# A two-layer diffusion block: modulation vectors of one stream, moved into the weights' load stream

## The chip, the cores and the metric

One core of a Trainium2 chip runs the whole program. The metric is device time in microseconds of that core, lower is better. The engines are named as in the profile: PE is TensorE (matmuls), PEld its weight loads, DVE is VectorE, ACT is ScalarE, POOL is GpSimd and SP is SyncE, which here only starts DMAs.

## The reference

Two layers over two streams of 256 tokens each, a latent stream x and a context stream, width 1024, all in float32. Each layer is FFN, mixer, FFN, and each of these three has a shift, a scale and a gate, nine modulation vectors of 1024 that are a matrix product of the conditioning vector with a large weight (ada_w):

```python
mod_x = (jax.nn.silu(c) @ ada_w[layer] + ada_b[layer]).reshape(b, N_MOD, 1, d)
mod_c = (jax.nn.silu(c_ctx) @ ada_w[layer] + ada_b[layer]).reshape(1, N_MOD, 1, d)
x = ffn_branch(x, mod_x, 0, norm_w[layer, 0], ffn_w1[layer, 0], ffn_w2[layer, 0])
ctx = ffn_branch(ctx, mod_c, 0, ...)
hx = ada_rms(x, norm_w[layer, 1], mod_x[:, 3], mod_x[:, 4])
hc = ada_rms(ctx, norm_w[layer, 1], mod_c[:, 3], mod_c[:, 4])
yx, yc = hybrid_mixer(hx, hc, ..., not last)
x = x + mod_x[:, 5] * yx
x = ffn_branch(x, mod_x, 6, norm_w[layer, 2], ffn_w1[layer, 1], ffn_w2[layer, 1])
if not last:
    ctx = ctx + mod_c[:, 5] * yc
    ctx = ffn_branch(ctx, mod_c, 6, ...)
```

The mixer is one input projection, three groups of heads (neighbourhood attention, a spatial gate, retention) and one output projection. Only x is returned. So in the last layer the vectors 5 to 8 (the mixer's gate, and shift, scale and gate of the last FFN) are needed for x alone.

## The kernel before

Activations lie transposed, feature on partitions, the two streams side by side in 512 columns. Every product is made of three matmuls of a high and a low part (wh, wl of the weights; hTh, hTl, aTh, aTl of the activations).

The weights come through one `Stream` (line 48): a list of chunks of up to 128x1024, in the order of their use. Three steps work along the list: `_load` starts a DMA on SP into one of three buffers `wr` (line 82), `_high` makes `wh` on ACT (line 92), and `_split` makes `wl` on DVE (line 103), whereupon the `wr` buffer is free. `take` hands a chunk to PE and then splits ahead until three chunks past it are split (`AHEAD`), and starts loads for three more. Instructions stand on each engine in the order in which the program is written (a manual schedule), so a step that waits holds what is written behind it on the same engine.

The first FFN of the first layer is called (0, 0) here, then come mixer 0, FFN (0, 1), FFN (1, 0), mixer 1 and FFN (1, 1). In an FFN each half has an up part (products `g`, `u`, some of them made by a faster scheme as `p`) and a down part (`d`). In a mixer the input projection has 28 chunks: three groups of four (`nat`, query, key and value), six `rqk`, then gates and spatial gate, and two `su` (in mixer 1 two chunks are swapped in order); 8 chunks of the output projection (`op`) follow.

The modulation vectors are 72 tiles of 128x1024 per layer (nine vectors by eight blocks). A tile is loaded by DMA and reduced on DVE against the conditioning vector `cb`, one multiply-and-sum per stream (line 293: a custom instruction and the reading of its sum); after eight blocks line 298 adds the bias, and where the vector is a scale or a half gate, one more small step follows. `ada_steps(l, count)` makes a list of such steps for as many reductions as `count` asks, and `pump`, called after each product, draws from that background list `bg` at a set pace. The table `ADA1` says how many reductions of the second layer stand in which FFN and half. For vectors 5 to 8 of the second layer a tile has one reduction, not two. There, in FFN (1, 0) and (1, 1), POOL starts the tiles' loads, into buffers of their own.

The mixers have background lists too: `qk_ticks` scales query and key (`qkn`, line 990) for PE's transposes (`qkt`, line 1003), attention follows (`sc`, `pt`, `o`), then retention, whose norm ends in POOL and DVE steps, and the spatial gate (`sg`). `windows` copies parts of the values on SP (`vW`, line 910), and mixer tables and biases are loaded on SP as well.

Of the kernel before, what the change touches and what calls it, by code (L numbers as in the profile page):

```python
# [43 lines left out]
ADA1 = {(0, 0): (40, 0), (0, 1): (16, 16), (1, 0): (16, 16), (1, 1): (8, 0)}  # L44
# [22 lines left out]
class Stream:  # L67
# [10 lines left out]
    def _load(self):  # L78
        i = self.n_load
        ap = self.chunks[i]  # L80
        t = self.pool.tile([128, CHUNK], F32, tag="wr", name="wr", bufs=RAW_BUFS)
        self.nc.sync.dma_start(out=t[:, : ap.shape[1]], in_=ap)
        self.raw[i] = t
        self.n_load += 1

    def _high(self):
        i = self.n_high
        if self.n_load <= i:
            self._load()
        h = self.pool.tile([128, CHUNK], F32R, tag="wh", name="wh", bufs=HL_BUFS)  # L90
# [5 lines left out]
    def _split(self):  # L96
        i = self.n_split
        n = self.chunks[i].shape[1]
        if self.n_high <= i:
            self._high()  # L100
        t, h = self.raw.pop(i), self.high.pop(i)
# [25 lines left out]
    def take(self, ahead=AHEAD):  # L127
        while self.n_split <= self.n_take:
            self._split()
# [8 lines left out]
def tile_hybrid_dit(ctx: ExitStack, tc: tile.TileContext, t_x, t_c, t_cb, t_ada0, t_ada, t_adab, t_nw, t_w1, t_w2,  # L138
# [83 lines left out]
    with tc.manual_schedule():  # L222
# [42 lines left out]
        ada_todo = [[(r, b) for r in range(2 if l == 0 else 0, 9) for b in range(KT)] for l in range(L)]  # L265

        def ada_steps(l, count):
# [3 lines left out]
            def streams(r):  # L271

                return 1 if l == L - 1 and r > 4 else 2

            todo = []
            while ada_todo[l] and sum(streams(r) for r, b in todo) < count:
# [11 lines left out]
            def step(i, s, n):  # L288
# [3 lines left out]
                junk = adap[3].tile([128, CHUNK], F32, tag="cu", name="junk", bufs=1) if s < n - 1 else t  # L292
                V.tensor_tensor_reduce(out=junk, in0=t, in1=cb[:, s], scale=1.0, scalar=0.0, op0=ALU.mult, op1=ALU.add,  # L293
                                       accum_out=mod[l][:, 8 * r + b, s:s + 1])

            def fin(r, n):
                mo = mod[l][:, 8 * r:8 * r + 8, 0:n]
                V.tensor_tensor(out=mo, in0=mo, in1=adab[:, l, 8 * r:8 * r + 8].unsqueeze(2).to_broadcast([128, KT, n]),
                                op=ALU.add)
                i, k = divmod(r, 3)  # L300
                if k == 1:
                    V.scalar_tensor_tensor(out=amul[l][:, i, :, 0:n], in0=mo, scalar=1.0,
                                           in1=nw[:, l, i, :].unsqueeze(2).to_broadcast([128, KT, n]),
                                           op0=ALU.add, op1=ALU.mult)
                elif k == 2 and i != 1:
                    V.tensor_scalar(out=mo, in0=mo, scalar1=0.5, scalar2=None, op0=ALU.mult)

            out = [lambda: loads(adap[1])]
            for i, (r, b) in enumerate(todo):
                n = streams(r)  # L310
                out += [lambda i=i, s=s, n=n: step(i, s, n) for s in range(n)]
                if b == KT - 1:
                    out.append(lambda r=r, n=n: fin(r, n))
# [324 lines left out]
        def ffn(l, f, lead, norms, steps=None, tail=None):  # L638
# [7 lines left out]
            with ExitStack() as es:  # L646
# [15 lines left out]
                else:  # L662
                    nb = ADA_BUFS - one
                    adap[:] = lambda i: fp.tile([128, CHUNK], F32, tag="aw", name="aw", bufs=nb), nb, G if one else SP, fp
                if one:
                    bg.extend([lambda: None] * 8 + ada_steps(1, ADA1[l, f][0]))
                    pace[0], pace[1] = len(bg) / (KT * (JH - 1)), 0.0
                for half in range(2):
# [121 lines left out]
                    if one and half == 0:  # L790
                        drain_bg()
# [1110 lines left out]
```

## Time and profile before

| | us |
|---|---|
| three timed runs | 1790.5, 1792.3, 1798.3 (median 1792.3) |
| the profiled execution | 1793.3 |
| its span in the trace | 1791.6 |
| PE busy | 1755.4 |
| DVE busy | 1294.0 |
| ACT busy | 719.1 |
| POOL busy | 257.1 |

The 1.7 us between the profiled execution and its span lie around the traced instructions. The granted TensorE clock was 0.998 of full speed over the span. PE's busy time counts a matmul from its start to its modelled end, so a PE that is always busy can still be fed slowly; waits are told apart in the rows further down, where a bracket at the end of a line holds the idle time before it and what ended it.

The stages by the trace: mixer 0 from 409 to 686 us, FFN (0, 1) to 1040, FFN (1, 0) to 1397, mixer 1 to 1590, FFN (1, 1) to the end.

### The profile page before, as it was taken

The page shows a single profiled execution, that of the slowest core. Times are in us where ns is not written, and L with a number is a line of the kernel's source. Part 1 is how long each engine was busy: PE and PEld are TensorE (multiplying, and loading weights), DVE is VectorE, ACT ScalarE, POOL GpSimd, SP SyncE. Part 2 cuts the span into 40 slices and gives each one's busy share as a digit, 9 for nine tenths or more (in the row PEclk, how much of TensorE's full clock was granted, in tenths as well). Part 3 has the DMA queues.
Part 4 walks back from the last instruction along what each step waited for, and adds up shares of the span by engine and source line. Part 5 has one row for each costly group of instructions (what it writes and reads, how often), then busy time and mean ns, then how long its engine had stood idle before and what let it go on. Part 6 is the DMA issues. An engine that isn't in the chain of part 4 may idle for free. (4 is left out here: it accounts for less than half of the span.)

```text
span 1791.6 us, 29394 instructions
## 1 busy us (share of the span) xinstructions
PE 1755.4 (98%) x11496; PEld 1544.3 (86%) x11496; DVE 1294.0 (72%) x2208; ACT 719.1 (40%) x1203; POOL 257.1 (14%) x307
## 2 busy tenths in 40 slices
PE   7999999999999999999999999999999999999999
PEld 5788888888678989898999899979998878899999
DVE  5789988986455567787688877776888745568665
ACT  3332222225544234442344244413542554454443
POOL 0000000002114400220322002113221105310000
PEclk9999999999999999999999999999999999999999
DMA  8756766644221122655775427567757432366655
GB/s 306 238 193 215 252 214 200 213 139 152 84 65 55 53 76 77 161 170 182 173 187 166 157 83 176 151 205 188 188 172 246 141 96 77 109 198 203 197 180 151
DMA packets 106811, 290.61 MB, mean 162 GB/s; under 512 B 12720, under 2 KB 22064, under 8 KB 106544
## 3 DMA queue, kind: packets, MB, share of 16 engines
q1 hardware_dynamic: 89392, 243.64, 41.9%
q0 software_dynamic: 17280, 45.10, 11.1%
q8 instruction: 90, 1.47, 0.3%
q14 instruction: 49, 0.40, 0.1%
HBM read 286.07 MB, written 1.05 MB: 160 GB/s over the span
## 5 line engine op out<-in xcount | busy, mean ns | idle before, releaser
L103 DVE TENSOR_TENSOR wl<-wr,wh 128x1024 fp32r<-128x1024 f32 (+2 forms) x308 | 325.7, 1083 | 108.3 <-ACT wh L92 107.2
L92 ACT CAST wh<-wr 128x1024 fp32r<-128x1024 f32 (+2 forms) x308 | 279.9, 934 | 185.1 <-PE d L210 88.9
L211 PE MATMUL d<-aTh,wl 128*128 128x512 f32 (+1 forms) x770 | 268.9, 349 | 2.5 <-DVE wl L103 2.5
L209 PE MATMUL d<-aTh,wh 128*128 128x512 f32 (+1 forms) x770 | 269.0, 349 | 0.7 <-ACT wh L92 0.7
L210 PE MATMUL d<-aTl,wh 128*128 128x512 f32 (+1 forms) x770 | 268.6, 349 | 0.0
L211 PEld LDWEIGHTS d<-aTh,wl 128*128 128x128 f32 x770 | 144.5, 188 | 24.6 <-DVE wl L103 3.5
L293 DVE CUSTOM_DVE_ANT_0 aw<-aw,cb 128x1024 f32<-128x1024 f32 x128 | 155.6, 1223 | 12.6 <-DMA aw<-in_ada_dram 9.9
L209 PEld LDWEIGHTS d<-aTh,wh 128*128 128x128 f32 x770 | 144.5, 188 | 22.1 <-ACT wh L92 0.9
L210 PEld LDWEIGHTS d<-aTl,wh 128*128 128x128 f32 x770 | 144.5, 188 | 21.2
L209 PE MATMUL g<-hTh,wh 128*128 128x512 f32 (+2 forms) x464 | 158.4, 341 | 2.1 <-ACT wh L92 1.1
L211 PE MATMUL g<-hTh,wl 128*128 128x512 f32 (+2 forms) x464 | 157.3, 339 | 2.0 <-DVE wl L103 2.0
L210 PE MATMUL g<-hTl,wh 128*128 128x512 f32 (+2 forms) x464 | 157.3, 339 | 1.3 <-DVE hTl L369 1.1
L211 PE MATMUL u<-hTh,wl 128*128 128x512 f32 (+2 forms) x464 | 156.4, 337 | 0.4 <-DVE wl L103 0.4
L209 PE MATMUL u<-hTh,wh 128*128 128x512 f32 (+2 forms) x464 | 156.1, 336 | 0.0
L210 PE MATMUL u<-hTl,wh 128*128 128x512 f32 (+2 forms) x464 | 156.1, 336 | 0.0
L217 PE MATMUL nat<-wh,hTh 128*128 128x512 f32 (+2 forms) x384 | 136.4, 355 | 0.0
L219 PE MATMUL nat<-wh,hTl 128*128 128x512 f32 (+2 forms) x384 | 128.4, 334 | 0.4 <-DVE hTl L369 0.4
L218 PE MATMUL nat<-wl,hTh 128*128 128x512 f32 (+2 forms) x384 | 128.3, 334 | 0.0
L293 DVE CUSTOM_DVE_ANT_0 junk<-aw,cb 128x1024 f32<-128x1024 f32 x96 | 117.0, 1219 | 4.0 <-DMA aw<-in_ada_dram 3.6
L595 PE MATMUL p<-hTh,wl 128*128 128x256 f32 x408 | 116.1, 285 | 0.7
L595 PE MATMUL p<-th,wl 128*128 128x256 f32 x408 | 114.7, 281 | 0.8 <-DVE wl L564 0.8
L594 PE MATMUL p<-hTl,wh 128*128 128x256 f32 x408 | 114.6, 281 | 0.0
(266 smaller groups left out, 4010.3 us busy)
## 6 DMA issues: line engine op xcount, KB each, us to landing
wr<-in_w_dram SPq DMA_DIRECT2D x142, 512.0 KB, 4.4
aw<-in_ada_dram SPq DMA_DIRECT2D x92, 512.0 KB, 4.9
wr<-in_wi_dram SPq DMA_DIRECT2D x56, 512.0 KB, 3.6
aw<-in_ada_dram POOLq DMA_DIRECT2D x52, 512.0 KB, 4.8
wr<-in_w_dram SPq DMA_DIRECT2D x64, 384.0 KB, 3.7
wr<-in_w_dram SPq DMA_DIRECT2D x64, 320.0 KB, 3.0
q<-in_w_dram SPq DMA_DIRECT2D x68, 256.0 KB, 3.7
q<-in_w_dram POOLq DMA_DIRECT2D x68, 256.0 KB, 5.3
```

Of the source, the lines that this page charges most:

```text
L92: self.nc.scalar.copy(out=h[:, :n], in_=self.raw[i][:, :n])
L103: self.nc.vector.tensor_tensor(out=lo[:, :n], in0=t[:, :n], in1=h[:, :n].bitcast(F32), op=ALU.subtract)
L209: PE.matmul(out=ps, lhsT=wh[:, col:col + 128], rhs=hh[rhs_sl], start=start, stop=False)
L210: PE.matmul(out=ps, lhsT=wh[:, col:col + 128], rhs=hl[rhs_sl], start=False, stop=False)
L211: PE.matmul(out=ps, lhsT=wl[:, col:col + 128], rhs=hh[rhs_sl], start=False, stop=stop)
L217: PE.matmul(out=ps, lhsT=hh[lhs_sl], rhs=wh[:, wc], start=start, stop=False)
L218: PE.matmul(out=ps, lhsT=hh[lhs_sl], rhs=wl[:, wc], start=False, stop=False)
L219: PE.matmul(out=ps, lhsT=hl[lhs_sl], rhs=wh[:, wc], start=False, stop=stop)
L293: V.tensor_tensor_reduce(out=junk, in0=t, in1=cb[:, s], scale=1.0, scalar=0.0, op0=ALU.mult, op1=ALU.add, accum_out=mod[l][:, 8 * r + b, s ...
L594: PE.matmul(out=ps, lhsT=wh[:, cw], rhs=tl, start=False, stop=False)
L595: PE.matmul(out=ps, lhsT=wl[:, cw], rhs=th, start=False, stop=n == 3)
```

## The change

The tiles of vectors 5 to 8 of the second layer become entries of the weights' stream. Behind each input projection chunk from the fourth on stands one such tile: 24 (vectors 5, 6, 7) in mixer 0, behind chunks 4 to 27, and 8 (vector 8) in mixer 1, behind chunks 4 to 11. An entry of this kind is loaded into a `wr` buffer by SP, has no ACT step, and in the place of the split it is reduced on DVE; `take` steps over it. They count in `AHEAD` and in the three buffers like any chunk. `ada_steps` now covers vectors 0 to 4 of the second layer alone; in `ADA1` FFN (1, 0) keeps 8 reductions (four tiles, both streams) in its first half and none in its second, and FFN (1, 1) has none. The work is the same in sum: 32 loads and 32 reductions have moved.

```diff
-ADA1 = {(0, 0): (40, 0), (0, 1): (16, 16), (1, 0): (16, 16), (1, 1): (8, 0)}
+ADA1 = {(0, 0): (40, 0), (0, 1): (16, 16), (1, 0): (8, 0)}
...
     def _load(self):
         i = self.n_load
         ap = self.chunks[i]
+        if isinstance(ap, tuple):
+            ap = ap[0]
...
     def _high(self):
...
+        if isinstance(self.chunks[i], tuple):
+            self.n_high += 1
+            return
...
     def _split(self):
         i = self.n_split
-        n = self.chunks[i].shape[1]
         if self.n_high <= i:
             self._high()
+        if isinstance(self.chunks[i], tuple):
+
+            self.chunks[i][1](self.raw.pop(i))
+            self.n_split += 1
+            return
...
     def take(self, ahead=AHEAD):
+        while isinstance(self.chunks[self.n_take], tuple):
+            self.split_to(1)
+            self.n_take += 1
...
+    between = [[(r, b) for r in v for b in range(KT)] for v in ((5, 6, 7), (8,))]
...
-                chunks += [t_wi[l, i] for i in WI[l]] + [t_wo[l, m] for m in range(KT)]
+                for n, i in enumerate(WI[l]):
+                    chunks.append(t_wi[l, i])
+                    if n >= 3 and between[l]:
+                        r, b = between[l].pop(0)
+                        chunks.append((t_ada[L - 1, r, b], lambda t, r=r, b=b: one_stream(r, b, t)))
...
+        def one_stream(r, b, t):
+            ada_step(L - 1, r, b, 0, t, t)
+            if b == KT - 1:
+                ada_fin(L - 1, r, 1)
...
-                if one:
-                    bg.extend([lambda: None] * 8 + ada_steps(1, ADA1[l, f][0]))
-                    pace[0], pace[1] = len(bg) / (KT * (JH - 1)), 0.0
```

PE's instructions and their order are the same in both. On SP, in mixer 1, around its first copies of values: `wr` buffers fed from `in_wi_dram` are weights, those from `in_ada_dram` modulation tiles. Before:

```order
L82 DMA wr_13597<-in_wi_dram 128x1024
L82 DMA wr_13615<-in_wi_dram 128x1024
L1461 DMA tab_13405<-in_tab_dram 128x1796
L910 DMA vW_13400<-yR_13402 64x128 x8
L82 DMA wr_13664<-in_wi_dram 128x1024
L82 DMA wr_13696<-in_wi_dram 128x1024
```

Now:

```order
L84 DMA wr_13610<-in_ada_dram 128x1024
L84 DMA wr_13625<-in_wi_dram 128x1024
L1479 DMA tab_13421<-in_tab_dram 128x1796
L928 DMA vW_13416<-yR_13418 64x128 x8
L84 DMA wr_13674<-in_ada_dram 128x1024
L84 DMA wr_13677<-in_wi_dram 128x1024
L84 DMA wr_13709<-in_ada_dram 128x1024
```

Ahead of the table and the eight copies stood the loads of ten weight chunks; now those of seven chunks and three tiles stand there, and the fourth tile (13674) comes behind the copies.

On DVE, in the same part of mixer 1: `wl` rows are splits, `qkn` rows the scaling of keys. Before:

```order
L990 TENSOR_TENSOR qkn_13398<-qkn_13398,qr_13561 128x384
L103 TENSOR_TENSOR wl_13694<-wr_13597,wh_13692 128x1024
L990 TENSOR_TENSOR qkn_13398<-qkn_13398,qr_13630 128x384
L103 TENSOR_TENSOR wl_13735<-wr_13615,wh_13733 128x1024
L990 TENSOR_TENSOR qkn_13398<-qkn_13398,qr_13645 128x384
```

Now:

```order
L1008 TENSOR_TENSOR qkn_13414<-qkn_13414,qr_13577 128x384
L113 TENSOR_TENSOR wl_13707<-wr_13625,wh_13705 128x1024
L290 ISA wr_13674,mod1_94<-wr_13674,cb_97 128x1024
L290 ISA mod1_94 128x1
L1008 TENSOR_TENSOR qkn_13414<-qkn_13414,qr_13640 128x384
L113 TENSOR_TENSOR wl_13751<-wr_13677,wh_13749 128x1024
L290 ISA wr_13709,mod1_94<-wr_13709,cb_97 128x1024
L1008 TENSOR_TENSOR qkn_13414<-qkn_13414,qr_13655 128x384
```

A reduction (two rows, ISA) now stands between each split and the scaling behind it.

On DVE, at the end of mixer 0's input projection, where the layer norm of the spatial gate runs (`v`, `sm`, `ss`). Before:

```order
L878 TENSOR_TENSOR v_5321<-v_5321,r_5474 128x512
L103 TENSOR_TENSOR wl_5494<-wr_5218,wh_5492 128x1024
L859 TENSOR_REDUCE sm_5502<-v_5321 128x8
...
L878 TENSOR_TENSOR v_5321<-v_5321,r_5516 128x512
L103 TENSOR_TENSOR wl_5540<-wr_5330,wh_5538 128x1024
L103 TENSOR_TENSOR wl_5572<-wr_5420,wh_5570 128x1024
L1566 SCALAR_TENSOR_TENSOR hTl_92<-yt_5580,gnw_89,hTh_91 128x512
```

Now:

```order
L896 TENSOR_TENSOR v_5377<-v_5377,r_5538 128x512
L113 TENSOR_TENSOR wl_5558<-wr_5389,wh_5556 128x1024
L113 TENSOR_TENSOR wl_5564<-wr_5479,wh_5562 128x1024
L877 TENSOR_REDUCE sm_5572<-v_5377 128x8
...
L896 TENSOR_TENSOR v_5377<-v_5377,r_5586 128x512
L113 TENSOR_TENSOR wl_5610<-wr_5484,wh_5608 128x1024
L113 TENSOR_TENSOR wl_5616<-wr_5560,wh_5614 128x1024
L113 TENSOR_TENSOR wl_5648<-wr_5566,wh_5646 128x1024
L1584 SCALAR_TENSOR_TENSOR hTl_92<-yt_5656,gnw_89,hTh_91 128x512
```

The split behind the first norm step was that of the second output projection chunk (5494); now the second `su` chunk's (5558) and the first output projection chunk's (5564) stand there, and three splits instead of two ahead of `hTl`.

## Rows read from the trace of the kernel before

**Rows 1.** Page, busy us, share of the span, instructions: each engine.

```profile
PE 1755.4 (98%) x11496; PEld 1544.3 (86%) x11496; DVE 1294.0 (72%) x2208; ACT 719.1 (40%) x1203; POOL 257.1 (14%) x307
```

**Rows 2.** Timeline (start, us, engine, line), DVE, last FFN, first and second half.

```profile
1638.78 2.36 DVE L103 TENSOR_TENSOR wl<-wr,wh 128x1024 fp32r<-128x1024 f32 x2 [0.52 <-ACT wh L92]
1641.06 1.22 DVE L293 CUSTOM_DVE_ANT_0 aw<-aw,cb 128x1024 f32<-128x1024 f32 x1
...
1642.20 1.22 DVE L293 CUSTOM_DVE_ANT_0 aw<-aw,cb 128x1024 f32<-128x1024 f32 x1
...
1646.31 2.36 DVE L103 TENSOR_TENSOR wl<-wr,wh 128x1024 fp32r<-128x1024 f32 x2 [0.52 <-ACT wh L92]
...
1707.11 2.36 DVE L103 TENSOR_TENSOR wl<-wr,wh 128x1024 fp32r<-128x1024 f32 x2 [0.53 <-ACT wh L92]
...
1712.92 2.36 DVE L103 TENSOR_TENSOR wl<-wr,wh 128x1024 fp32r<-128x1024 f32 x2 [0.53 <-ACT wh L92]
```

**Rows 3.** Groups by form (ns min/median/max, first and last start), down halves, last FFN.

```profile
L209 PE MATMUL d<-aTh,wh x88: 278/278/280, 1660.7 to 1692.5; 128*128 128x256 f32 x88
...
L209 PE MATMUL d<-aTh,wh x88: 277/280/280, 1756.8 to 1787.2; 128*128 128x256 f32 x88
```

**Rows 4.** Windows of PE: length, busy; FFN (0, 1) and FFN (1, 0).

```profile
804.48:866.24 61.76, 61.76 (x268) 1.00 0.64 186
1157.80:1221.32 63.52, 62.02 (x268) 1.00 0.68 208
866.08:976.67 110.59, 110.37 (x926) 1.00 0.62 161
1221.16:1334.17 113.01, 111.80 (x926) 1.00 0.63 160
```

**Rows 5.** Timeline of DVE, first down half of FFN (1, 0).

```profile
1202.98 1.23 DVE L293 CUSTOM_DVE_ANT_0 aw<-aw,cb 128x1024 f32<-128x1024 f32 x1 [3.20 <-DMA aw<-in_ada_dram]
```

**Rows 6.** Timeline of SP's queue (start, us from first to last issue), mixer 1.

```profile
1420.69 0.42 SPq L1461 DMA_DIRECT2D tab<-in_tab_dram  x1
1421.16 8.11 SPq L910 DMA_DIRECT2D vW<-yR  x8
1429.37 7.78 SPq L82 DMA_DIRECT2D wr<-in_wi_dram  x4
```

**Rows 7.** Page, DMA issues: KB each, median us to landing.

```profile
wr<-in_wi_dram SPq DMA_DIRECT2D x56, 512.0 KB, 3.6
```

**Rows 8.** Timeline of DVE, mixer 1, the third scaling.

```profile
1427.02 0.55 DVE L990 TENSOR_TENSOR qkn<-qkn,qr 128x384 f32<-128x384 f32 x1
```

**Rows 9.** Timeline of PE, mixer 1, transposes.

```profile
1431.48 0.49 PE L1003 MATMUL qkt<-ident,qkn 128*128 128x128 f32 x3
...
1433.47 0.51 PE L1003 MATMUL qkt<-ident,qkn 128*128 128x128 f32 x3
...
1441.41 0.55 PE L1003 MATMUL qkt<-ident,qkn 128*128 128x128 f32 x3 [0.91 <-DVE qkn L990]
```

**Rows 10.** Windows: length, then busy of PE, PEld, DVE, ACT, POOL; mixer 0.

```profile
409.00:623.00 214.00, 212.52 (x1469) 173.85 (x1470) 118.00 (x275) 97.45 (x208) 59.78 (x70) 1.00 0.26 81
```

**Rows 11.** Timeline of DVE and of PE, mixer 0, second group of chunks.

```profile
437.33 1.23 DVE L103 TENSOR_TENSOR wl<-wr,wh 128x1024 fp32r<-128x1024 f32 x1 [2.74 <-ACT wh L92]
...
441.60 0.40 PE L217 MATMUL nat<-wh,hTh 128*128 128x512 f32 x1
```

**Rows 12.** Timeline of ACT and of PE, mixer 0, attention.

```profile
485.01 0.22 ACT L1187 ACTIVATE ww<-ww 128x24 f32<-128x24 f32 x1 [1.83 <-DVE ww L1185]
...
487.00 0.34 PE L1111 MATMUL o<-pt,vW 128*64 128x64 f32 x4 [1.26 <-ACT pt L1085]
```

**Rows 13.** Timeline of PE and DVE, end of mixer 0's input projection.

```profile
629.75 0.40 PE L211 MATMUL su<-hTh,wl 128*128 128x512 f32 x1
...
630.45 1.22 DVE L103 TENSOR_TENSOR wl<-wr,wh 128x1024 fp32r<-128x1024 f32 x1
...
640.27 0.98 PE L1413 MATMUL sg<-sgw,v 128*64 128x128 f32 x14 [0.89 <-DVE hTl L1566]
```

More of the change, by code (lines that the diff above doesn't have):

```diff
@@ L97, in _split @@
         i = self.n_split
-        n = self.chunks[i].shape[1]
         if self.n_high <= i:
             self._high()
+        if isinstance(self.chunks[i], tuple):
+            self.chunks[i][1](self.raw.pop(i))
+            self.n_split += 1
+            return
+        n = self.chunks[i].shape[1]
         t, h = self.raw.pop(i), self.high.pop(i)
@@ L163, in tile_hybrid_dit @@
             if f == 1:
-                chunks += [t_wi[l, i] for i in WI[l]] + [t_wo[l, m] for m in range(KT)]
+                for n, i in enumerate(WI[l]):
[3 more added lines that the diff above has]
+                        chunks.append((t_ada[L - 1, r, b], lambda t, r=r, b=b: one_stream(r, b, t)))
+                assert not between[l]
+                chunks += [t_wo[l, m] for m in range(KT)]
             for half in range(2):
@@ L286, in loads, with step @@
                     nload[0] += 1
-            def step(i, s, n):
+            def step(i, s):
                 loads(i + adap[1])
@@ L291, in step @@
                 t = tiles[r, b]
[L292 to L306, printed above, removed]
+                ada_step(l, r, b, s, t, t if s else adap[3].tile([128, CHUNK], F32, tag="cu", name="junk", bufs=1))
             out = [lambda: loads(adap[1])]
             for i, (r, b) in enumerate(todo):
-                n = streams(r)
-                out += [lambda i=i, s=s, n=n: step(i, s, n) for s in range(n)]
+                out += [lambda i=i, s=s: step(i, s) for s in range(2)]
                 if b == KT - 1:
-                    out.append(lambda r=r, n=n: fin(r, n))
+                    out.append(lambda r=r: ada_fin(l, r, 2))
             return out
@@ L662, in ffn @@
                 else:
-                    nb = ADA_BUFS - one
-                    adap[:] = lambda i: fp.tile([128, CHUNK], F32, tag="aw", name="aw", bufs=nb), nb, G if one else SP, fp
-                if one:
-                    bg.extend([lambda: None] * 8 + ada_steps(1, ADA1[l, f][0]))
-                    pace[0], pace[1] = len(bg) / (KT * (JH - 1)), 0.0
+                    adap[:] = lambda i: fp.tile([128, CHUNK], F32, tag="aw", name="aw", bufs=ADA_BUFS), ADA_BUFS, SP, fp
                 for half in range(2):
@@ L789, in ffn @@
                     split_tail = half == 1 and len(streams) == 2
-                    if one and half == 0:
-                        drain_bg()
                     if seven:
```

20 lines of the change are left out of this document (16 added, 4 removed).

## The prediction

> **What bounds the kernel now.** I read the page's busy times first: TensorE (PE) is busy 1755.4 us, 98% of the span [rows 1]. So time moves in two ways only: a PE wait that goes, or a PE wait that comes. The change leaves PE's instructions as they are, word for word and in order; it moves 32 loads of 512 KB and 32 reductions on VectorE (DVE) from the second layer's two FFNs into the two mixers. I therefore read, stage by stage, what PE loses beside those reductions now, and how much room DVE and the load queue have where they go.
>
> **What it takes away: second layer, last FFN.** 8 reductions run in its first half, in pairs behind each pair of weight splits. One costs DVE 1.15 us, start to start (1641.06 to 1642.20), since the reading of its sum overlaps the next instruction [rows 2]. With two of them a pair of splits comes every 7.53 us (1638.78 to 1646.31); in the second half, with none, every 5.82 (1707.11 to 1712.92). PE can't run faster than its splits, and two such pairs (the second, to 1653.84, repeats the first) come after its lead is used up: 2 x 1.71 = 3.4 us. The down projection behind it shows the rest: its first matmuls run from 1660.7 to 1692.5 in the first half, from 1756.8 to 1787.2 in the second, 31.8 against 30.4, 1.4 us [rows 3]. I take 4.8.
>
> **What it takes away: second layer, first FFN.** The same FFN with the same pools runs one stage earlier, as the first layer's last. There the first down half takes 61.76 us and the second up half 110.59; in the second layer 63.52 and 113.01 [rows 4]. The difference, 1.8 + 2.4, is what I credit. For the first a row shows the cause: tiles that one stream alone reads are used up twice as fast, and at 1202.98 DVE stood 3.20 us for its tile's DMA, with the split that PE needed behind it [rows 5]. After the change 4 tiles with two reductions each are left there, half the rate of the first layer's 8. That the 2.4 goes too is inferred (the same PE work, the preceding stage calm); if not, the gain is smaller by it. The 16 reductions of the second half stand beside no PE loss and give nothing back. Taken away together: 4.8 + 1.8 + 2.4 = 9.0 us; bounds 5 (direct waits and rhythm, without most of what is compared) and 10.
>
> **What it adds: second mixer, 8 reductions.** The order shows where they fall: one behind each split, ahead of the scaling (qkn) that PE's next transposes need. And the loads now stand in SP's own queue, with fewer ahead of the first block of vW copies: three modulation tiles and weights to the seventh chunk, where ten chunks' weights stood. SP is held there: a table load at 1420.69, eight vW issues from 1421.16 for 8.11 us, the next weight load only at 1429.37 [rows 6]. The fourth modulation tile now takes that slot. With the median landing of an input projection load, 3.6 us [rows 7], it is there at 1433.0; its reduction ends at 1434.15. Behind it on DVE stands the scaling that ran at 1427.02 for 0.55 us [rows 8]: it now ends at 1434.7. PE's transposes at 1431.48 need it [rows 9]: 3.2 us late. Then DVE owes a split, a reduction and a scaling (1.15 + 1.15 + 0.55). The split waits for a weight load issued just after the tile and then cast, so it starts about 1435.5, my estimate from 1429.37, 3.6, one more issue and a cast; the chain ends at 1438.4. The transposes at 1433.47, by then due at 1436.7, wait 1.7 more. Last, the transposes at 1441.41 already wait 0.91 for the scaling, with nothing between split and scaling; a reduction stands there now: 1.15 straight onto PE [rows 9]. Sum 3.2 + 1.7 + 1.1 = 6.1 us (rounded up). Bounds: 2, if the load isn't held behind vW, and 8, with 1.3 us later landing and its followers.
>
> The Trainium skill, DMA: Bandwidth & Descriptors, section "Issuing engines are not separate DMA queues", says that DMAs run on the same 16 engines whichever engine starts them, so that starting them from several saves the starting engine's time alone. By that, moving loads from GpSimd's queue to SP's would change little more than issue time, and this mixer would cost 2.0. The 8.11 us in which SP starts no load [rows 6] is such sequencer time, but not small; I go by the row.
>
> **What it adds: first mixer, 24 reductions.** In 409 to 623 us DVE is busy 118.0 of 214 us [rows 10]; 24 x 1.15 = 27.6 makes 146, 68%. So no shortage, only lateness. Two places where lateness has no cover. (a) At 485.01 ScalarE waited 1.83 us for DVE's ww step, which follows a split directly; behind it on ScalarE stands the copy for which PE waits 1.26 us at 487.00 [rows 12]. A reduction comes between: 1.15. (b) The end. The split of the second su chunk now stands where that of the chunk two later stood: 630.45, held by layer norm steps [rows 13]; with half a microsecond from the reductions ahead, 630.95 to 632.1. PE's third matmul of that chunk needs it at 629.75: 2.4. Then three splits instead of two stand ahead of the hTl step for which PE waits at 640.27 already (0.89): lateness 0.5 + 1.15 + 1.15 = 2.8 in all, 0.4 more than the 2.4 that PE has lost by then. For the other 22 places I allow 1.5, an estimate, a twentieth of the 27.6: the split itself has room. Ahead of each chunk the stream still splits three entries, but every second is a modulation tile, so a chunk's split stands where that of the chunk two later stood: the one at 437.33 ends at 438.56, and the chunk that now uses it starts at 441.60 [rows 11], 3.0 us of cover against 1.15 of lateness. Sum 1.15 + 2.8 + 1.5 = 5.5 us; bounds 1 and 10.
>
> **The sum.** 9.0 off, 6.1 + 5.5 on: +2.6 us. The profiled execution took 1793.3 us (span 1791.6), 1.0 above the median of the three timed runs. 1793.3 + 2.6 = 1796 us (by the median, 1795).
>
> **The rivals.** (A) The mixers swallow the reductions: DVE idles nearly half the time there [rows 10], and loads land before they are needed. Against it: four places where PE waits for DVE with no cover. It gives 1793.3 - 9.0 = 1784. (B) The fourth tile isn't late in the second mixer, because the loads land as from another queue or vW goes through faster: 1793.3 - 9.0 + 2.0 + 5.5 = 1792; the Trainium skill's section named above would have it so. For it: nothing in the rows but that sentence's own logic; against it: 8.11 us. (C) Slower: in the first mixer the reductions wait for their own loads, as at 1202.98. Each entry has one of three buffers, so a tile's load starts when the preceding chunk's split ends, one chunk ahead (some 8 us: 24 chunks in 430 to 629). It decides where a load takes more than those 8 us: then DVE stands, 3.2 us as there [rows 5], plus 1.15, less 3.0 of cover, 1.35 on PE per chunk; at half of the 24 chunks 16 us: 1796 + 16 = 1812. Against it: 3.6 us landing [rows 7]; for it: copies and bias loads share SP. (D) The change doesn't give back what the FFNs lose, because their waits have another cause: only 1.4 of the 9.0 comes, 1804. Against it: rows 2 show the reductions inside the longer rhythm.
>
> **How the numbers follow.** Forecast 0.52, A 0.12, B 0.15, C 0.13, D 0.08. Range 1786 to 1805: it takes in B, D, the bounds on each side (5 to 10 off, 3 to 18 on, not all at one end) and leaves out C and half of A. A difference under 0.5% (9 us) can't be told from no change here. Faster by more than that: half of A, 0.06. Slower: C, half of D and the forecast's far end, 0.18. Within: 0.76.
>
> **What would show it.** Right: PE waits of about 3 and 2 us at the qkt transposes some 30 us into the second mixer, with DVE standing for a DMA on its fourth reduction; a wait of about 2.4 at su and of 3 or more, all told, at su and sg; in the last FFN a pair of splits every 5.8 us in both halves; first down half and second up half of the FFN before at 61.8 and 110.6. Wrong: PE waits spread over all chunks of the first mixer (C), none at qkt (A, B), or the old lengths in the FFNs (D).

## The result, and the profile after

The changed kernel takes 1807.22 us (median of four runs, 1805.85 to 1809.23), the kernel before 1793.05 beside it: a ratio of 1.0076, interval 1.0062 to 1.0089. It is 14.2 us slower where 2.6 had been forecast, and 2.2 us beyond the range.

The page of after begins with the line that [rows 1] shows of before:

```profile
span 1806.8 us, 29383 instructions
PE 1763.4 (98%) x11496; PEld 1550.8 (86%) x11496; DVE 1298.4 (72%) x2208; ACT 717.3 (40%) x1203; POOL 247.8 (14%) x275
```

The span grew by 15.2 us, and PE's busy time by 8.0 with the same 11496 instructions. Half of the loss is therefore no waiting: the same matmuls took longer. The windows of the two mixers show where, first before, then after (stretch, its length, PE's busy time, granted clock, DMA share, GB/s). The cuts lie at the same PE instruction in both kernels, within some 7 us of a stage's first product, so they differ a little from the bounds that the section on the profile before gives:

```profile
409.29:680.88 271.59, 269.22 (x1801) 1.00 0.26 80
1400.08:1596.71 196.63, 188.63 (x1357) 0.98 0.37 115
```

```profile
412.50:695.90 283.40, 273.31 (x1801) 0.99 0.38 122
1410.90:1616.93 206.03, 193.74 (x1357) 0.96 0.41 130
```

Length less busy time is waiting. With the other stages cut in the same way:

| stage, us | before | after | length | of it waiting | of it PE's busy time |
|---|---|---|---|---|---|
| FFN (0, 0) | 409.3 | 412.5 | +3.2 | +0.7 | +2.5 |
| mixer 0 | 271.6 | 283.4 | +11.8 | +7.7 | +4.1 |
| FFN (0, 1) | 362.9 | 362.9 | 0.0 | | |
| FFN (1, 0) | 356.3 | 352.1 | -4.2 | -2.5 | -1.7 |
| mixer 1 | 196.6 | 206.0 | +9.4 | +4.3 | +5.1 |
| FFN (1, 1) to the end | 194.9 | 189.9 | -5.0 | -3.0 | -2.0 |

The two FFNs gave back 9.2 us, the mixers took 21.2. FFN (0, 0) is untouched by the change; its length varies from run to run, which the next section shows.

**The FFNs did what was forecast.** Windows of PE in the first down half and the second up half of FFN (1, 0), to set beside [rows 4], and the splits of the last FFN's first half, beside [rows 2]:

```profile
1172.80:1234.56 61.76, 61.76 (x268) 1.00 0.54 155
1234.39:1344.99 110.60, 110.39 (x926) 1.00 0.62 159
```

```profile
1656.66 2.36 DVE L113 TENSOR_TENSOR wl<-wr,wh 128x1024 fp32r<-128x1024 f32 x2 [0.52 <-ACT wh L97]
1662.47 2.36 DVE L113 TENSOR_TENSOR wl<-wr,wh 128x1024 fp32r<-128x1024 f32 x2 [0.52 <-ACT wh L97]
```

61.76 and 110.60 are the lengths that the first layer showed, and a pair of splits comes every 5.81 us.

**The mixers waited where it was forecast, and at more places.** PE in mixer 0 (start, us, engine, line; in brackets the wait before it and what ended it); [rows 12, 13] have the first and the last of these places before; at the second, among the neighbourhood blocks, PE waited 0.22 us before, at the third not at all:

```profile
492.51 0.34 PE L1129 MATMUL o<-pt,vW 128*64 128x64 f32 x4 [2.40 <-ACT pt L1103]
...
546.29 1.08 PE L1071 MATMUL sc<-qkT 64*64 64x256 f32 x8 [1.36 <-ACT sc L1079]
...
641.25 0.50 PE L230 MATMUL su<-hTh,wh 128*128 128x512 f32 x1 [1.36 <-ACT wh L97]
...
644.29 0.79 PE L232 MATMUL su<-hTh,wl 128*128 128x512 f32 x1 [2.31 <-DVE wl L113]
```

And mixer 1: SP's queue, DVE's reduction of the fourth tile, and the transposes, beside [rows 6, 8, 9]:

```profile
1431.11 8.04 SPq L928 DMA_DIRECT2D vW<-yR  x8
1439.24 0.54 SPq L84 DMA_DIRECT2D wr<-in_ada_dram  x1
```

```profile
1443.13 1.23 DVE L290 CUSTOM_DVE_ANT_0 wr<-wr,cb 128x1024 f32<-128x1024 f32 x1 [5.07 <-DMA wr<-in_ada_dram]
```

```profile
1444.98 0.52 PE L1021 MATMUL qkt<-ident,qkn 128*128 128x128 f32 x3 [2.10 <-DVE qkn L1008]
...
1459.51 0.84 PE L1021 MATMUL qkt<-ident,qkn 128*128 128x128 f32 x3 [2.05 <-DVE qkn L1008]
```

The load of the fourth tile starts when SP is through with the copies, DVE stands 5.07 us for it, and the transposes wait.

**What had no term in the sum: the clock behind those waits.** Windows of PE in after (the third number from the end is the granted clock):

```profile
490.00:495.00 5.00, 2.60 (x20) 0.87 0.71 234
495.00:500.00 5.00, 5.00 (x31) 0.79 0.13 33
640.00:645.00 5.00, 1.45 (x4) 0.88 0.00 0
645.00:650.00 5.00, 5.00 (x19) 0.77 0.64 210
1445.00:1450.00 5.00, 4.76 (x22) 0.60 0.83 225
1450.00:1455.00 5.00, 5.00 (x23) 0.72 0.59 207
...
1460.00:1465.00 5.00, 5.00 (x23) 0.70 0.61 216
```

Behind each of these long waits part of the next five to ten us runs at the lower of TensorE's two levels (1.2 instead of 2.4 GHz). That is most of the 4.1 and the 5.1 us of busy time that came on top in the mixers. How much of it made the kernel longer is another question, for PE may have waited instead; e2_fill answers it.

### The profile page after: what moved, and what is told of

It reads as the page before. It is cut to its first block, busy times and chain, and to the rows that moved or that the text cites. A ratio compares the mean times of both kernels' runs of the same rounds, so it can differ in the third digit from the quotient of the medians.

```text
span 1806.8 us, 29383 instructions
## 1 busy us (share of the span) xinstructions
PE 1763.4 (98%) x11496; PEld 1550.8 (86%) x11496; DVE 1298.4 (72%) x2208; ACT 717.3 (40%) x1203; POOL 247.8 (14%) x275
## 5 line engine op out<-in xcount | busy, mean ns | idle before, releaser
L290 DVE CUSTOM_DVE_ANT_0 aw<-aw,cb 128x1024 f32<-128x1024 f32 x96 | 117.4, 1223 | 2.5
```

What stands on the lines that cost most here:

```text
L290: V.tensor_tensor_reduce(out=out, in0=t, in1=cb[:, s], scale=1.0, scalar=0.0, op0=ALU.mult, op1=ALU.add, accum_out=mod[l][:, 8 * r + b, s: ...
```

## The experiments

Each kernel was timed beside the kernel before. The lengths are those of its profiled execution, cut as above (271.6, 196.6, and 356.3 for FFN (1, 0), in the kernel before).

| kernel | us | before | ratio (interval) | mixer 0 | mixer 1 | FFN (1, 0) |
|---|---|---|---|---|---|---|
| e5_after, the changed one again | 1808.91 | 1792.25 | 1.0088 (1.0073 to 1.0103) | 283.4 | 203.8 | 352.1 |
| e1_none | 1786.94 | 1794.27 | 0.9961 (0.9947 to 0.9975) | 271.6 | 195.8 | 352.1 |
| e2_fill | 1804.88 | 1794.27 | 1.0064 (1.0047 to 1.0081) | 282.1 | 204.8 | 352.1 |
| e4_before_fill | 1797.63 | 1794.27 | 1.0024 (1.0015 to 1.0034) | 271.5 | 199.2 | 354.5 |
| e6_vw_behind | 1813.01 | 1792.25 | 1.0107 (1.0087 to 1.0127) | 283.4 | 211.7 | 352.1 |
| e9_one_copy | 1801.56 | 1793.52 | 1.0046 (1.0031 to 1.0060) | 283.1 | 201.0 | 352.1 |
| e14_before_one_copy | 1795.01 | 1794.26 | 1.0005 (0.9995 to 1.0015) | 271.5 | 195.7 | 355.0 |
| e3_late | 1809.40 | 1794.27 | 1.0090 (1.0075 to 1.0106) | 283.3 | 207.2 | 352.1 |
| e7_ahead | 1810.28 | 1792.25 | 1.0097 (1.0081 to 1.0113) | 280.4 | 211.5 | 352.1 |
| e8_where_room | 1789.75 | 1792.25 | 0.9977 (0.9965 to 0.9988) | 275.4 | 195.8 | 352.1 |
| e10_two_earlier | 1792.64 | 1793.52 | 0.9993 (0.9983 to 1.0003) | 277.1 | 198.2 | 352.1 |
| e11_ahead_too | 1794.32 | 1793.52 | 1.0005 (0.9996 to 1.0015) | 279.0 | 195.8 | 352.1 |
| e12_quarter | 1795.65 | 1792.97 | 1.0016 (1.0008 to 1.0025) | 272.2 | 195.7 | 362.9 |
| e13_combined | 1789.24 | 1794.26 | 0.9977 (0.9966 to 0.9987) | 272.3 | 200.3 | 352.1 |

### The gain alone, and the changed kernel once more

```
-    between = [... for v in ((5, 6, 7), (8,))]
+    between = [... for v in ((), ())]
...   (and the 32 vector blocks are set to zero)
```

> The changed kernel without its 32 moved entries: the 32 loads and reductions stand neither in the FFNs nor in the mixers (second-layer modulation vectors 5 to 8 are left out, set to zero instead). So it shows what taking them out of the FFNs gives, by itself. Theory 1 (the FFNs gave all that was forecast and the two mixers took it back and more, by waits and by the low clock behind them): 9.2 us under the kernel before, 1784, with both mixers as long as in the kernel before (mixer 0 from its first nat product to the first product of the FFN behind it 280 us, mixer 1 196.6). Rival (rest of the change, such as the later start of the first FFN by 3.2 us, belongs to the new program and not to the moved entries): about 1787, with the first FFN 3 us longer.

The mixers are as long as before and FFN (1, 0) and FFN (1, 1) have lost their 9.2 us; the ratio says 7.0, between 4.5 and 9.5. So the gain is real and the loss lies wholly in the 32 entries of the mixers. FFN (0, 0) took 414.3 us here, the longest of all sixteen traces, so this run does not settle whether the new program starts later; the next bears on it:

> The changed kernel once more, beside the three variants of it, so that they are compared on one chip. 1807, and a second trace of it: the first FFN, in which its trace was 3.2 us longer than that of before although nothing is changed there, should by theory 1 (that difference belongs to the run, not to the program) come out anywhere within some 4 us; by the rival (the new program starts later) 3 us longer again. The granted clock may fall behind other waits than in the first trace, if the fall behind a wait of 1.3 to 3.7 us is a matter of chance.

FFN (0, 0), where all these kernels are alike, took between 408.5 and 414.3 us. The kernel before and its two variants had 409.3, 410.9 and 414.0, the changed one 412.5 and 413.5, and two variants of the changed one (e3_late, e6_vw_behind) 409.6 and 411.2. So nothing speaks for its 3.2 us belonging to the program. The second trace also shows that the clock's part changes from run to run: it fell behind su and behind the second wait of 2.05 at the transposes again, but not behind the one at the fourth neighbourhood block (2.40) nor behind the first at the transposes (1.93), and mixer 1 took 203.8 instead of 206.0 us.

### The clock behind a wait

```
+        def fill(ps, n):
+            for k in range(n):
+                PE.matmul(out=ps, lhsT=hTh[:, 0, 0:128], rhs=hTh[:, 0, 0:ps.shape[1]], start=True, stop=True)
...
+                    if (l, b) == (0, 1):
+                        fill(ps, 14)
...   (the same at the other places, with 18, 8 and 8)
```

> The changed kernel with extra matmuls whose results are overwritten, put on TensorE where it waited longest in the changed kernel's trace: 18 of 256 columns ahead of the weighted sum of the fourth neighbourhood block (wait 2.40 us), 14 of 512 ahead of the second su chunk (1.36 and 2.31), 8 each ahead of two groups of qkt transposes in mixer 1 (2.10 and 2.05). The waits themselves are not shortened, only filled. Theory 1 (TensorE ran at half its clock for some us behind each of these waits, 7.4 us in all by the shift between the two traces): the granted clock stays 1.00 there and the kernel is 7 us faster than the changed one, about 1800. Rival (the lost time lies in the waits alone, or the clock falls anyway): 1807, or slower by what the extra matmuls take.

The clock stayed up in every window in which it had fallen:

```profile
490.00:495.00 5.00, 4.93 (x44) 1.00 0.70 222
...
645.00:650.00 5.00, 5.00 (x26) 1.00 0.65 213
1445.00:1450.00 5.00, 3.63 (x25) 1.00 0.73 220
1450.00:1455.00 5.00, 5.00 (x30) 1.00 0.70 215
```

By the shift between the two traces this gave 1.2 us at the fourth neighbourhood block and 3.3 at the transposes. At su it gave next to nothing (0.2): what PE was faster there it waited for DVE at the sg products, where it had waited 0.89 before the change [rows 13] and not at all in after:

```profile
655.14 1.09 PE L1439 MATMUL sg<-sgw,v 128*64 128x128 f32 x16 [1.09 <-DVE hTl L1594]
```

So TensorE's pace was the limit in two of the three places, and DVE in the third. The lengths say what is left without the low clock behind the new waits: mixer 0 is still 10.5 us longer than before, and mixer 1 8.2, of which 1.5 went by chance: behind the yt transposes of mixer 1 the clock fell in this trace and not in that of after, though PE had waited 1.82 us in both. PE's timeline and a window in e2_fill, then the window behind the same wait in after:

```profile
1586.92 0.44 PE L1591 MATMUL yt<-ident,yR 128*128 128x128 f32 x2 [1.82 <-POOL yR L1373]
```

```profile
1585.00:1590.00 5.00, 3.18 (x18) 0.74 0.23 88
```

```profile
1590.00:1595.00 5.00, 5.00 (x44) 1.00 0.01 3
```

Without these 1.5 the two mixers lost 10.5 + 6.7 = 17.2 us to DVE's and the loads' lateness alone, and the low clock cost 21.2 - 17.2 = 4.0 us of the first trace. In time the runs don't tell this kernel clearly from the changed one (1.0064 against 1.0076 and 1.0088, with intervals that overlap); the traces do, at the places themselves.

> The kernel before, with 14 extra matmuls of 512 columns whose results are overwritten, ahead of the sg products of mixer 1, where TensorE waited 3.55 us and ran at a granted clock of 0.56 and 0.76 in the ten us behind. Theory 1 (the low clock follows from the wait): clock 1.00 there, 3.4 us faster than before, about 1789.5. Rival (the clock falls for another reason, such as the work of the other engines, or the extra matmuls make the wait longer): 1793 or more.

This kernel tests neither theory. The wait at sg is one for the PSUM bank, which the extra matmuls write too, so they stood behind the wait instead of in it: they read hTh alone and still came only after 3.60 us:

```profile
1546.76 4.96 PE L264 MATMUL sg<-hTh 128*128 128x512 f32 x14 [3.60 <-DVE sd L1302]
```

Fourteen of them took 4.96 us, where in e2_fill fourteen of the same shape took 3.38. So the low clock meets whatever follows the wait, needed work or not, and the extra matmuls only cost time.

### Mixer 1: the copies in SP's queue

```
-                if last:
-                    windows(0, 128)
...   (nat_group of the second product group, behind its first take:)
+                            if mid and ci == 0:
+                                mid()
```

> The changed kernel with mixer 1's table load and its first eight vW copies issued from SP after the next weight and tile loads instead of ahead of them; everything else stands. Theory 1 (the fourth tile's load was late because it stood behind those copies in SP's queue): the tile lands some 4 us earlier, the 5.07 us that DVE stood for it go, the waits of 2.10 and 0.24 us at the qkt transposes go, with 3 us of low clock behind them: mixer 1 about 5 us shorter than in the changed kernel, 1802. Rival (the transfers share the same 16 engines, so the order of the issues changes little): the tile lands when it did, 1807.

The tile landed in time, and the transposes that had waited 2.10 us waited no more. But the copies still hold SP for 8.79 us, and now the next tile stood behind them:

```profile
1435.63 8.79 SPq L928 DMA_DIRECT2D vW<-yR  x8
1444.52 0.53 SPq L84 DMA_DIRECT2D wr<-in_ada_dram  x1
```

```profile
1450.20 0.87 PE L1023 MATMUL qkt<-ident,qkn 128*128 128x128 f32 x3 [6.58 <-DVE qkn L1010]
```

The place of the wait follows the order in SP's queue: the mechanism is right, the cure wrong. So the copies were taken out of the second product group:

```
-                if last:
-                    windows(0, 128)
-                windows(128 if last else 0, 256)
+                windows(0, 256)
```

> The changed kernel with mixer 1's first two groups of vW copies (eight issues of 128 columns ahead of the second product group, eight behind it) made into one group of eight of 256 columns behind the second product group. The first copies only stood ahead of the loads; nothing reads them before the neighbourhood blocks. Theory 1 (the 8 us in which SP's queue issues those copies make the fourth tile late; moved behind one take, as in the preceding variant, they only make the next load late): no load waits behind them in the second product group, the waits of 2.10 and 0.24 us at the qkt transposes and the low clock behind them go, and no new one of 6 us comes as there: mixer 1 some 4 to 6 us shorter than in the changed kernel, 1802 to 1804. The wait of 2.05 at the qkt transposes after that stays at 0.9 to 2, a reduction stands ahead of its scaling. Rival (it is the three loads in a row that saturate the DMA engines): the tile lands as late, 1808.

5 to 8 us below the changed kernel (1.0046 against 1.0076 and 1.0088), mixer 1 at 201.0 us, of which the clock behind yt, which fell in this trace, is 1.5. The tile's load is issued 4.6 us behind the load ahead of it instead of 9.0, and only the wait with the reduction straight ahead of the scaling is left, at its old size:

```profile
1432.18 0.33 SPq L84 DMA_DIRECT2D wr<-in_ada_dram  x1
```

```profile
1440.02 0.49 PE L1021 MATMUL qkt<-ident,qkn 128*128 128x128 f32 x3
...
1442.29 0.52 PE L1021 MATMUL qkt<-ident,qkn 128*128 128x128 f32 x3
...
1451.39 0.55 PE L1021 MATMUL qkt<-ident,qkn 128*128 128x128 f32 x3 [2.06 <-DVE qkn L1008]
```

The control, the same edit in the kernel before:

> The kernel before with the one group of vW copies behind the second product group, nothing else changed: the control for that edit. Theory 1 (the copies held up only the moved tiles' loads; ten chunks' weights stood ahead of them in the kernel before): within 1.5 us of the kernel before. Rival (the edit is worth 7 us by itself, and the variant of the changed kernel showed that and not the tiles' wait): 1786.

No difference beyond 2 us (1.0005, 0.9995 to 1.0015). So the copies cost nothing until the tiles stood behind them. The tiles can also be moved, behind later chunks:

```
-                        if n >= 3 and between[l]:
+                        if n >= (3, 12)[l] and between[l]:
```

> The changed kernel with mixer 1's eight tiles behind its chunks 12 to 19 instead of 3 to 10, so that no load of a tile stands behind the vW copies in SP's queue and no reduction stands ahead of a qkn scaling. Theory 1 (SP's queue, and reductions on the path to the qkt transposes, made mixer 1 longer by 9.4 us, half of it by the low clock): mixer 1 back to 197 to 199 us, total about 1799. Rival (DVE has no room for the eight reductions wherever they stand in mixer 1): the waits move to the later products, mixer 1 still 203 us or more, total 1804 to 1808.

Both theories were half right. The waits at the transposes went, but mixer 1 took 207.2 us, since the retention has no room on DVE either:

```profile
1520.94 1.83 PE L1336 MATMUL ro<-rv,sd 128*128 128x64 f32 x12 [2.18 <-DVE sd L1312]
...
1538.03 0.39 PE L239 MATMUL nat<-wl,hTh 128*128 128x256 f32 x1 [2.56 <-DVE wl L113]
```

### Mixer 0: how far the stream looks ahead

```
-        while self.n_split < min(self.n_take + ahead, self.cap):
+        upto = self.n_take
+        while upto < len(self.chunks) and ahead > 0:
+            ahead -= not isinstance(self.chunks[upto], tuple)
+            upto += 1
+        while self.n_split < min(upto, self.cap):
```

> The changed kernel with the stream looking three chunks ahead again, tiles not counted, as in the kernel before; buffers as they are. Theory 1 (in mixer 0 the second su chunk and its successors came late since a chunk's split stood where that of the chunk two later had stood): the waits of 1.36 and 2.31 us at su go, and mixer 0 is 3 to 5 us shorter; at the neighbourhood blocks the 1.1 us behind ww stay, since a reduction stands ahead of ww still. Mixer 1, where tiles now have to land earlier, 0 to 5 us longer. In all 1803 to 1809. Rival (DVE is late there by the sum of its work, not by the order of it): the waits at su stay within a microsecond, and the total with them.

The waits at su went altogether, with the low clock behind them. The one at the fourth block is 1.26 us, what it was before the change [rows 12], so the expectation that it would stay was wrong: on DVE the reduction that stood between the split and ww now stands ahead of the split, in time in which DVE would have waited for ScalarE's cast. Three smaller ones (0.69, 0.53, 0.25) went with it. PE:

```profile
437.84 0.79 PE L242 MATMUL nat<-wh,hTh 128*128 128x512 f32 x1 [2.97 <-ACT qkn L981]
...
495.51 0.34 PE L1133 MATMUL o<-pt,vW 128*64 128x64 f32 x4 [1.26 <-ACT pt L1107]
...
546.91 1.08 PE L1075 MATMUL sc<-qkT 64*64 64x256 f32 x8 [1.60 <-ACT sc L1083]
...
651.33 1.09 PE L1435 MATMUL sg<-sgw,v 128*64 128x128 f32 x16 [0.91 <-DVE hTl L1588]
```

Some 5.4 us of mixer 0's 7.7 were thus those of a shorter lead; three waits among the later neighbourhood blocks, 0.52, 0.53 and the 1.60 above, stayed, so the lead is not their cause (that it is the reductions themselves is inferred). By length it is more: from the first of these waits (465.60 in before) to its end mixer 0 is 2.6 us longer than before here, and 10.5 in e2_fill. But the lead has to be built up first: with six entries on three buffers ScalarE's casts wait for loads, the copies that free PE's banks wait behind them, and PE waits 2.97 us at the start, with the low clock behind it, 6.2 us in all. Mixer 0 won 3.0 us of 11.8, and mixer 1 lost 5.5, more than expected; the whole took 1.3 us more than the range expected.

### Where the moved work costs nothing

```
-ADA1 = {(0, 0): (40, 0), (0, 1): (16, 16), (1, 0): (8, 0)}
+ADA1 = {(0, 0): (40, 0), (0, 1): (16, 16), (1, 0): (8, 16)}
-    between = [... for v in ((5, 6, 7), (8,))]
+    between = [... for v in ((5, 8), ())]
-                    if n >= 3 and between[l]:
+                    for k in range(2 if n >= 16 and between[l] else 0):
...   (vectors 6 and 7 are reduced in the FFN again, for one stream)
```

> Only half of the move: vectors 6 and 7 (16 tiles) stay in the second half of the second layer's first FFN, as in the kernel before; vectors 5 and 8 go into mixer 0 alone, two tiles behind each of its chunks 16 to 23 (the end of the retention projections and the gates), none in mixer 1. Theory 1 (the 16 reductions of the second half cost nothing where they were; in the changed kernel's trace no wait stands in mixer 0 between 548 and 639 us, so DVE has room there): the FFNs' 9.2 us are kept and the mixers lose 0 to 2, total 1785 to 1788. Rival (DVE has no room in a mixer wherever the tiles stand): mixer 0 some 5 us longer or more, 1791 or more.

Faster than before by 0.23% (0.12 to 0.35), though between the two theories' times, and the FFNs kept their gain with 16 reductions still in the second half. What mixer 0 lost, 3.8 us, begins on DVE with three splits in a row, where one had stood (1.23 us at 614.22 in before), ahead of the layer norm steps; PE's wait at sg grows from 0.89 to 3.16:

```profile
616.21 3.50 DVE L113 TENSOR_TENSOR wl<-wr,wh 128x1024 fp32r<-128x1024 f32 x3 [1.91 <-ACT wh L97]
```

```profile
644.54 1.77 PE L1435 MATMUL sg<-sgw,v 128*64 128x128 f32 x16 [3.16 <-DVE hTl L1588]
```

> As the half move (vectors 6 and 7 stay in the FFN; 5 and 8 in mixer 0, two tiles behind each chunk), but behind chunks 14 to 21 instead of 16 to 23. There, three weight splits stood in a row at 616.21, where the stream made up its lead after the last tile, two more than before ahead of the layer norm chain that ends at the sg products, and TensorE waited 3.16 us there instead of 0.89. Theory 1 (those two splits, 2.3 us, are the whole loss, and the low clock of some 1.5 us came with it): with the lead made up two chunks earlier the sg wait is back at 0.9 to 1.5, mixer 0 as long as in the kernel before within 1.5 us, total 1784 to 1787. Rival (the tiles take DVE time from the chain wherever they stand in the gates): the sg wait stays at 3, total 1790.

The wait at sg is back at 0.90 us, but the earlier tiles now reach into the neighbourhood blocks: PE waits 0.91 and 2.51 us there, and mixer 0 is longer than in e8_where_room. Neither theory held.

> As the half move (chunks 16 to 23), with the stream looking three chunks ahead, tiles not counted. Theory 1 (the stream's lead decides): nothing to make up behind the last tile, the sg wait back at 0.9; but at the first tiles the lead has to grow by six entries on three buffers, so a wait of some 1 to 3 us there: 1786 to 1789. Rival: sg wait still 3, 1790.

The wait at sg is 0.88 us, as expected. Building up the lead cost more than expected, 5.6 us in four waits between 521 and 544 us, and low clock behind the last.

> A quarter of the move: only vector 5 (8 tiles) goes into mixer 0, two tiles behind each of its chunks 18 to 21, so after the neighbourhood blocks and two chunks before the su chunks; vectors 6, 7 and 8 (24 tiles) stand in the second half of the second layer's first FFN, where 16 stood in the kernel before. Theory 1 (that half has room on DVE; in mixer 0 the only room is between the neighbourhood blocks and the layer norm chain ahead of su): the FFNs' 9.2 us stay, no wait is added in either mixer, total 1783 to 1786. Rival (24 tiles of 512 KB in that half come too late, as its first half's did in the kernel before, or the splits of the down half wait for them): that FFN's second down half, 55.46 us from its first to its last product, becomes 2 us longer or more, total 1787 to 1790.

Two answers. Eight tiles between the neighbourhood blocks and the layer norms are free: mixer 0 took 272.2 us. Twenty-four reductions in the FFN's second half are not: its last down half takes 66.28 us instead of 55.46. Neither a load nor a split is what PE waits for longest there: DVE runs four reductions in a row, its step on the down product (xT, line 482) stands behind them, ScalarE waits 6.57 us for that step, and the cast that PE needs stands behind it on ScalarE:

```profile
1389.21 0.81 ACT L368 ACTIVATE sq<-xT 128x256 f32<-128x256 f32 x2 [6.57 <-DVE xT L482]
...
1390.80 0.58 PE L230 MATMUL d<-aTh,wh 128*128 128x256 f32 x1 [3.81 <-ACT wh L97]
```

> Vector 5 in mixer 0, two tiles behind each of its chunks 18 to 21 (no loss in the preceding variant); vectors 6 and 7 in the second half of the second layer's first FFN, as in the kernel before; vector 8 in mixer 1 behind chunks 3 to 10 as in the changed kernel, but with one group of vW copies behind the second product group. Theory 1 (the parts add: 9.2 us off in the FFNs, mixer 0 as before, in mixer 1 only what the variant with one group of copies kept, 2 to 3 us): 1785 to 1788, faster than both kernels. Rival (the parts disturb one another, or mixer 1 keeps more): 1790 or more.

The parts add: FFN (1, 0) 352.1, mixer 0 272.3, mixer 1 200.3 (a wait of 2.42 us at the transposes is left, and a low clock behind yt). 4 to 5 us faster than the kernel before beside it (0.9977, 0.9966 to 0.9987), though 1.2 us over what was expected; with e8_where_room it is the best of these.

## Why the prediction was wrong, point by point

**The FFNs, 9.0 us: right, in each term.** 61.76 and 110.60 us are the two lengths of [rows 4] that were read off the first layer; the last FFN gave 5.0 for the 4.8 forecast. (One reduction costs 1.14 us by its two rows, not 1.15; nothing hangs on it.) e1_none shows it without the mixers. Rival (D) falls.

**First failed step, mixer 0: its lateness, 5.5 us forecast, 10.5 measured.** The waits that were named came, and counted as waits the stage looks near: 7.7 for 5.5. But e2_fill, where the clock stayed at 1.00 through all of mixer 0, still has it 10.5 us longer. Term by term:

- (a), behind ww: 2.40 instead of 1.26, 1.14 for 1.15, and in the trace of after the reduction stands on DVE between the split and ww, as forecast. Right.
- (b), at su and sg: the waits sum to 1.36 + 2.31 - 0.89 = 2.8 for 2.8, but this agreement is luck. The stretch is 4.4 us longer in e2_fill, as DVE's chain is in after, from the first step of the layer norms to `hTl`, 28.8 us before and 33.2 after; in after PE spent the rest in matmuls at the low clock. The two more splits are worth the 2.3 forecast. The reductions ahead of them, taken at half a microsecond, made DVE 2.1 us late, for two of them now stand among the norm's steps. Timeline of DVE, before, then after:

```profile
610.70 0.68 DVE L859 TENSOR_REDUCE sm<-ro 128x8 f32<-128x512 f32 x1
...
639.47 1.40 DVE L1566 SCALAR_TENSOR_TENSOR hTl<-yt,gnw,hTh 128x512 fp32r<-128x512 f32 x2
```

```profile
621.14 0.68 DVE L877 TENSOR_REDUCE sm<-ro 128x8 f32<-128x512 f32 x1
...
625.80 1.22 DVE L290 CUSTOM_DVE_ANT_0 wr<-wr,cb 128x1024 f32<-128x1024 f32 x1
...
632.80 1.77 DVE L290 CUSTOM_DVE_ANT_0 wr<-wr,cb 128x1024 f32<-128x1024 f32 x1
...
654.31 1.40 DVE L1584 SCALAR_TENSOR_TENSOR hTl<-yt,gnw,hTh 128x512 fp32r<-128x512 f32 x2
```

- "For the other 22 places I allow 1.5", since "the split itself has room": 4.9 by length in e2_fill, 3.8 as waits in after, nearly all in six of 0.25 to 1.36 us among the neighbourhood blocks.

The prediction saw that the lead shortens and judged the cover sufficient. By e7_ahead it was not: with the lead of three chunks the part behind the build-up lost 2.6 us instead of 10.5. DVE never stood for a tile's load in mixer 0, so the mechanism of rival (C) isn't what made it slow, though its 1812 lies nearer to the measured 1807 than the forecast's 1796. (A) falls: the mixers lost 21.2 us.

**Mixer 1, 6.1 us forecast: right in mechanism, and in size without the clock.** e2_fill has it 6.7 us longer, the fall behind yt left out. As waits it was 4.3 in the first trace. The third grew by 1.14 (forecast 1.15). The first was 2.10 for 3.2: relative to PE, SP reached the copies some 1.3 us sooner than before, for a reason that was not followed (ten loads stand ahead of them in both kernels; the prediction's "fewer" counts weights alone). The second was 0.24 for 1.7, since PE, at the low clock, came later itself; in e5_after, where the clock stayed up there, it is 1.19. Rival (B) falls by e6_vw_behind, e9_one_copy and e14_before_one_copy: the order in SP's queue alone moved 5 to 8 us. The Trainium skill, DMA: Bandwidth & Descriptors, section "Issuing engines are not separate DMA queues", would have made this mixer cost 2.0; the issuing time that it calls usually small was 8.04 us here and decided.

**Second failed step: the first sentence.** "Time moves in two ways only: a PE wait that goes, or a PE wait that comes" took PE's busy time as fixed. It grew by 9.2 us in the mixers in the first trace and by 5.9 in the second (mixer 0 3.7, mixer 1 2.2). Not all of that made the kernel longer, for where DVE was late PE would have waited instead: by e2_fill the low clock cost 4.0 us of the first trace, and by the same sum 1.8 of the second. This is in part why the waits, 11.6 forecast and 12.0 measured, agree, which is luck: a slower PE waits less for a late DVE. The one window of a mixer among the rows, [rows 10], shows a clock of 1.00, and none of mixer 1 was read for it. The trace of before had the row that would have shown the price: at 1546.92 PE had waited 3.55 us in mixer 1, and behind that the windows read

```profile
1545.00:1550.00 5.00, 3.08 (x21) 0.56 0.31 105
1550.00:1555.00 5.00, 5.00 (x36) 0.76 0.00 0
```

a loss of (1 - 0.56) x 5 + (1 - 0.76) x 5 = 3.4 us, some of it during the wait itself, behind a wait of 3.55. In proportion, an estimate, some 2 us behind each of the four longest waits foreseen (ww, su, two at the transposes) would have added 8 us, twice what the clock cost in the first trace.

The Trainium skill, TensorE: Matmul & The Clock Gate, section "HAM oscillation — how this bites in real kernels", describes it: a matmul engine that idles for want of data comes back at half its clock, and so pays for the wait a second time; in the section's example the waits are of about 3 to 5 us. The trace agrees on the fall, with 0.60 and 0.72 in the ten us behind the wait of 2.10, and shows it behind shorter waits than the example's.

**The whole.** The lateness alone, 17.2 us on for 9.2 off, would have given about 1801 from the 1793.3 of the profiled execution, within the range; the clock's 4.0 and the 3.2 of FFN (0, 0) make up the 1808.6 that the profiled execution of after took. By the stages other than FFN (0, 0) the change costs 12.0 us in the first trace (12.0 waiting and 9.2 of busy time on, 9.2 off) and 9.9 in the second; the medians say 14.2, with an interval of 11 to 16. The few us between are within what FFN (0, 0) alone varies, and aren't attributed further. The 21.2 us on lie beyond the 18 that the prediction's bounds allowed the mixers; the 17.2 of lateness don't. That a difference under 0.5% can't be told from no change was too cautious: the 0.23% of e8_where_room has an interval of 0.12 to 0.35.

## What to carry to other kernels

Read, for each wait of the busy engine, the granted clock behind it as well: here the low clock added 4.0 us to 17.2 in one trace, so an engine that is busy 98% of the time does not have a fixed busy time. A slower engine also waits less, so a sum of waits that comes out right proves little: compare the stages' lengths, and the chain of the engine that is late. When work goes into a stream with a fixed look-ahead, count what the look-ahead is worth in the old unit, and look at the places behind which it has to be made up. Moving work out of a stage gives back what the stage's rows promise; where it goes is to be chosen by the place, not by the share of the time in which the receiving engine is idle: 8 reductions were free in one stretch of mixer 0, and 16 that reached two to four chunks beyond it cost 4 to 6 us.

## What the runs showed of the hardware

- Whether the clock falls behind a wait is partly chance. At the yt transposes of mixer 1 all sixteen traces show a wait of 1.82 or 1.83 us, and the clock fell behind it in five, at a cost of 1.5 us. Behind the wait of 2.40 us at the fourth neighbourhood block it fell in one of the five traces that had it unfilled. Behind the wait at sg in mixer 1, 2.86 to 3.72 us, it fell in all fifteen that weren't filled. What decides it isn't shown.
- Eight copies of parts of the values (vW) hold SP's queue for 4.9 to 9.1 us, over all sixteen traces, and a load of 512 KB that stands behind them is issued only when they are through: at 1439.24 in after, 9.0 us behind the load ahead of it, where it is 4.6 in e9_one_copy.
- The first FFN, alike in all sixteen kernels, varied by up to 6 us between runs: in its first 35 us, where the matmuls reach full speed sooner or later (those of 128x512 took 0.63 us between 27 and 33 us in the trace of after, 0.39 to 0.40 mostly in that of before), and behind a wait of about 1 us near 395, where the clock fell in some runs.
